# Moving the split weights of the half-width products by 144 bytes (112 for paired values) inside their buffers

## The chip, the cores and the metric

The kernel runs on one core of one Trainium2 chip. The metric is the device time of one execution in microseconds (us); lower is better. One core has a matrix engine, TensorE (PE in the profile, with its weight loads listed apart as PEld), and four more engines: VectorE (DVE), ScalarE (ACT), GpSimd (POOL) and SyncE (SP, which only issues transfers here). On-chip memory is SBUF, 128 partitions wide; an address below is a byte offset within a partition. Matrix products land in PSUM.

## The reference, cut to what matters

A two-layer decoder trunk over 512 tokens of width 1024, all in float32:

- layer 0 mixes tokens by attention in three groups of eight heads, with windows of 128, 512 and 2048 tokens at strides 1, 4 and 16; the three groups' outputs are merged by their softmax denominators and projected;
- layer 1 mixes tokens by causal means over 2, 4, 8 and 16 positions, with one small linear map for each channel group;
- after each mixer comes a SwiGLU feed-forward block of hidden width 2816, and before every block an RMS norm.

```python
x = x + dilated_attention_mixer(rmsnorm(x, attn_norm), w_qkv, w_attn_out)   # layer 0
x = x + (silu(h @ gate) * (h @ up)) @ w_down                                # after each mixer
x = x + pooling_mixer(rmsnorm(x, pool_norm), w_pool_in, w_pool_group, scale) # layer 1
return rmsnorm(x, final_norm)
```

Nearly all of the arithmetic is in products of activations with weights that are read once from HBM.

## The kernel before, in words

**Split operands.** A float32 product is made of three TensorE products in the reduced type `fp32r`. Every operand is split into a high part (ScalarE copies it, rounded) and a low part (VectorE subtracts the high part from the original); `split` at L81 to L83 does it. Then high by high, high by low and low by high are summed in PSUM.

**Weights.** Weights arrive by transfer in `raw` buffers and are split into buffers of five in turn: `whi` and `wlo`, each 128 x 1024 (`halfhi` and `halflo`, 128 x 512, two in turn). The class `Held` takes such a buffer. Loads and splits stand in two lists, and `pump` issues the next of them after products, as soon as a buffer is free, so that the weights are split some products ahead of their use.

**Two kinds of products.** `Product` (L259, L260, L262) multiplies a 128 x 128 block of weights with 512 columns of activations. `seven` calls `mult` (L374 to L376): for two outputs at a time the eight quarter products are replaced by seven (Strassen's scheme, in a form that shares sums), and each of the seven is four blocks of 128 x 128 weights against 256 columns. `values12` (L488 to L490) does the same for two value projections with the operands' roles exchanged: there the activations are the stationary operand (the one that is loaded into the array) and the weights are the moving one, 256 columns wide. The class `Pair` loads the four quarters, forms their sums and splits four sets of weights ("b", "s", "m", "l"). In this text the products of `mult` and `values12` are the half-width products.

**Where things lie.** Activations that are split lie in slots of 128 x 2 x 512, in the buffers of `x`, or in some buffers of the attention's pool. In the program before, every slot and every weight buffer begins at an address that leaves 128 when divided by 256, and the blocks inside them begin at multiples of 512 (weights) or 1024 bytes (activations). So the stationary and the moving operand of each half-width product begin at the same remainder modulo 256. Two pads, each called `shift`, one in the pool of temporaries and one in the feed-forward pool, lie ahead of the slots.

**Sums of squares.** `square` (L288 on) forms the sum of squares for the next norm: ScalarE squares a chunk into `sq` (two buffers), and VectorE adds it to the sum so far in a new `acc` buffer (two buffers).

**Order.** Every engine runs its instructions in the order in which the program writes them. The order of the products is written out in the loops; the splits of later weights are put among them by `pump`.

Of the kernel before, what the change touches and what calls it, by code (L numbers as in the profile page):

```python
# [8 lines left out]
F32 = mybir.dt.float32  # L9
F32R = mybir.dt.float32r  # L10
# [5 lines left out]
P = 128  # L16
S = 512
# [26 lines left out]
DOWN = (6, 5)  # L44
BUFS = {"w": 5, "half": 2, "raw": 4, "rawhalf": 2}
COLS = {"w": D, "half": D // 2, "raw": D, "rawhalf": D // 2}
FIXED = 12
SLOTS = 15
QK = [(0, 0), (0, 1), (1, 0), (1, 1), (2, 0), (2, 1)]
# [4 lines left out]
def trunk(ctx: ExitStack, tc: tile.TileContext, xT, norms, w_first, w_qk, w_qkp, w_v0, w_v0p, w_v12, w_out, w_pair, w_down, w_pin, w_pgrp,  # L54
          consts, ident_in, invcnt_in, outT, outR):
    nc = tc.nc
    cpool = ctx.enter_context(tc.tile_pool(name="cpool", bufs=1))
    wpool = ctx.enter_context(tc.tile_pool(name="wpool", bufs=1))
    tmp = ctx.enter_context(tc.tile_pool(name="tmp", bufs=2))
# [21 lines left out]
    def split(hi, lo, v):  # L81
        nc.scalar.activation(hi, v, AF.Copy)  # L82
        nc.vector.tensor_tensor(lo, v, hi.bitcast(F32), op=OP.subtract)  # L83
# [3 lines left out]
    class Held:  # L87


        def __init__(self, ring):  # L90
            self.live = True
            n = COLS[ring]
            if ring in ("w", "half"):
                self.t = [wpool.tile([P, n], F32R, tag=ring + c, name=ring + c, bufs=BUFS[ring]) for c in ("hi", "lo")]
            else:
                self.t = wpool.tile([P, n], F32, tag=ring, name=ring, bufs=BUFS[ring])
            rings[ring].append(self)
# [28 lines left out]
    class Pair:  # L126

        def __init__(self, src):  # L130
            self.src, self.w = src, {}
            loads.append((self, {"raw": 2, "rawhalf": 1}, self.load))

        def steps(self):
# [8 lines left out]
                                self.src[:, None, 3 * S:].to_broadcast([P, 2, S]), accum_op=OP.add)  # L143

        def blocks(self):
            self.w["b"] = Held("w")
            split(*self.w["b"].t, self.a.t)

        def sums(self):
            self.w["s"] = Held("w")  # L150
            split(*self.w["s"].t, self.b.t)

        def more(self):
            a, b = self.a.t, self.b.t
            nc.vector.tensor_add(a[:, :S], a[:, :S], b[:, :S])
            nc.vector.tensor_add(a[:, S:], a[:, S:], a[:, :S])
            self.b.done()
            self.w["m"] = Held("w")
            split(*self.w["m"].t, a)
            self.a.done()  # L160

        def last(self):
            self.w["l"] = Held("half")
            split(*self.w["l"].t, self.c.t)
            self.c.done()

# [10 lines left out]
                return  # L177
            steps.popleft()[2]()

    def pairs(*srcs):  # L180

        these = [Pair(src) for src in srcs]
        for parts in zip(*(p.steps() for p in these)):
            steps.extend(parts)
        units.append(these)
# [5 lines left out]
    def plain(*srcs):  # L191
        units.extend([Plain(src) for src in srcs])

    for h in range(HEADS):
        if h == 0:
            plain(*[w_qk[u] for u in range(len(QK) - NF)])
        for g in range(3):
            if h == 1 and g < NSOLO:
                plain(*[w_qk[len(QK) - NF + 2 * g + c] for c in range(2)])
            elif h:  # L200
                pairs(w_qkp[3 * h - 3 - NSOLO + g])
        if h == 0:
            plain(w_v0[0], w_v0[1])
        elif h % 2 == 0:
            pairs(w_v0p[h // 2 - 1])
        else:
            pairs(w_v12[h // 2, 0], w_v12[h // 2, 1])
    plain(*[w_out[m] for m in range(KC)])

    def ffn_plan(layer):  # L210
# [20 lines left out]
    class Product:  # L231
# [16 lines left out]
        def add(self, ks, cols=slice(0, S), pos=None):  # L248
            for k in ks:
                if self.w:  # L250
                    w, c = self.w, k if pos is None else pos + k
                else:
                    held, c = self.where(k)
                    w = held.t
                    if c == self.sizes[len(self.tiles) - 1] - 1 and not self.keep:
                        held.done()
                s = slice(c * P, (c + 1) * P)
                mh, ml = self.ins(k)
                nc.tensor.matmul(self.p[:, cols], w[0][:, s], mh[:, cols], start=self.done == 0, stop=False)  # L259
                nc.tensor.matmul(self.p[:, cols], w[0][:, s], ml[:, cols], start=False, stop=False)  # L260
                self.done += 1
                nc.tensor.matmul(self.p[:, cols], w[1][:, s], mh[:, cols], start=False, stop=self.done == self.n)  # L262
            if not self.w:
                pump(2)
            return self


    free, pools = deque(range(FIXED)), {i: cpool for i in range(FIXED)}

# [18 lines left out]
    acc = {}  # L288

    def square(layer, k, engine=None):  # L290
        sq = tmp.tile([P, S], F32, name="sq")
        nc.scalar.activation(sq, X[k], AF.Square)
        if layer not in acc:
            acc[layer] = sq
            return
        new = tmp.tile([P, S], F32, name="acc")
        (engine or nc.vector).tensor_add(new, acc[layer], sq)
        acc[layer] = new

    def scaled(layer, k, hi, lo, on_dve=False):  # L300

# [8 lines left out]
    def note(layer, k):  # L310

        if layer < 4:
            held[layer, k], t = slot("h")
            scaled(layer, k, t[:, 0], t[:, 1])
        square(layer, k)
# [67 lines left out]
    def seven(T, one, two, scratch, after={}, blocks=False):  # L383
# [35 lines left out]
        if blocks:  # L419
            for a in (left, right):  # L420
                nc.vector.tensor_add(in_place(sums, a), in_place(p73, a), into(one, right))
        else:
            nc.vector.tensor_add(sums, p73, again(one[:, H2:]))
# [32 lines left out]
    with tc.tile_pool(name="opool", bufs=1) as opool:  # L456
        early = opool.tile([P, HEADS, S], F32R, tag="o", name="early")
        with tc.tile_pool(name="apool", bufs=1) as apool:
# [6 lines left out]
            def scaled_by(t, p, blocks):  # L465
                nc.vector.tensor_mul(by_block(t) if blocks else t, p, rows["row"])
# [292 lines left out]
            for k in range(KC):  # L759
                if k % 2 == 0:  # L760
                    rawh, wh = Held("raw"), Held("w")
                    rawh.done()
                    wh.done()
                    raw, (hi, lo) = rawh.t, wh.t
                s = slice(k % 2 * NF * P, (k % 2 + 1) * NF * P)
                nc.sync.dma_start(X[k], xT[:, k, :])
                nc.sync.dma_start(raw[:, s], w_first[k])
                nc.scalar.activation(hi[:, s], raw[:, s], AF.Copy)
                scaled(0, k, *U[k], on_dve=k == 0)
                nc.vector.tensor_tensor(lo[:, s], raw[:, s], hi[:, s].bitcast(F32), op=OP.subtract)  # L770
                for i, f in enumerate(lead):
                    f.w = (hi, lo)
                    f.add([k], pos=k % 2 * NF + i - k)
                square(0, k)
# [79 lines left out]
            output(last - 1)  # L854
            halve(last - 1)
            turn0(last)
            turn12(last)
            lead.append(Product(HEADS, heads).add(range(last - 1)))
            output(last)
            halve(last)  # L860
            for f in lead:
# [14 lines left out]
    with tc.tile_pool(name="fpool", bufs=2) as fpool:  # L876
        fpool.tile([P, 32], F32, name="shift", bufs=1)
        for i in range(FIXED, FIXED + SLOTS):
            free.append(i)
# [160 lines left out]
        def mix(g):  # L1040
            for c in range(2):
                f = Product(2, lambda k: Y[g][k], w=wg[g // 2, g % 2]).add(range(2), pos=2 * c)
                m = 2 * g + c
                nc.vector.scalar_tensor_tensor(X[m], f.p, nrm[:, 5, m:m + 1], X[m],
                                               op0=OP.mult, op1=OP.add)
                held[3, m], t = slot("n")
                scaled(3, m, t[:, 0], t[:, 1])
                square(3, m, nc.gpsimd)
            for c in range(2):
                give(("y", g, c))  # L1050
# [23 lines left out]
        def end(i, half, js, f=None):  # L1074
            f = f or Product(HALF, hidden, keep=ends[i])
            return f.add(js, cols=halves[half])
# [38 lines left out]
        def total(half, sq):  # L1115
            t = ftile("total", H2)
            nc.vector.tensor_add(t, acc[4][:, halves[half]], sq)
            return t

        t = total(0, add(0, 0, end(0, 0, range(HALF))))  # L1120
        sq = add(1, 0, end(1, 0, range(HALF)))
# [3 lines left out]
        t = total(1, add(0, 1, f))  # L1125
# [6 lines left out]
        sq = add(1, 1, f)  # L1132
# [90 lines left out]
```

## Time and profile before

| | |
|---|---|
| median of 3 runs | 1249.99 us (1249.98 to 1250.75) |
| span of the profiled execution | 1249.2 us |
| TensorE products, weight loads | 9294, 9294 |
| TensorE busy | 99% of the span |
| VectorE busy | 922.7 us, 74% |
| ScalarE busy | 569.4 us, 46% |
| granted TensorE clock | 0.999 of full |

The profile gives one profiled execution; no time of that execution other than its span is given. An instruction of TensorE is listed with its start and a duration; products are pipelined, so that a listed duration (283 ns for 256 columns) is longer than the distance from one start to the next (0.12 us). How quickly TensorE works is therefore read from the distances of the starts in the timeline, or from how many products fall into a stretch of time. The trace holds starts in whole nanoseconds; the timeline rounds them to 0.01 us. Names such as `ps<-tt,whi` say that a product into PSUM read the tile `tt` (split activations) and `whi` (high parts of weights).

### The profile page before, as it was taken

To read this page: it belongs to the slowest core of one execution; us is meant where nothing else is said; L and a number is where in the kernel's file an instruction comes from. 1 tells how busy PE (TensorE), PEld (TensorE's weight loads), DVE (VectorE), ACT (ScalarE), POOL (GpSimd) and SP (SyncE) were. 2 spreads that over 40 slices of the span, in tenths; PEclk is the share of its full clock that TensorE was granted. 3 is DMA by queue.
4 is the path that set the end of the run, shared out by engine and by line. 5 is a ranking of instruction groups with operands and counts; after the bars stand their busy time and mean duration, and the time that the engine had idled before them with its cause. 6 is when DMAs were issued, how large, how long until landed. Compare 5 with 4: busy or idle time off the path is not lost.

```text
span 1249.2 us, 23008 instructions
## 1 busy us (share of the span) xinstructions
PE 1238.6 (99%) x9294; PEld 1141.3 (91%) x9294; DVE 922.7 (74%) x1474; ACT 569.4 (46%) x923; POOL 123.5 (10%) x119
## 2 busy tenths in 40 slices
PE   9999999999999999999999999999999999999998
PEld 7889999999999988899889999888789988999987
DVE  6888887877879754889437886659888954788643
ACT  6545464545446552545324554443444632455331
POOL 1011121111111100000001100000400000111000
PEclk9999999999999999999999999999999999999999
DMA  8346565666665633356356763333135645676321
GB/s 288 113 111 154 142 160 154 165 151 150 155 155 146 208 108 100 79 135 179 111 143 176 184 169 119 110 129 119 51 85 119 183 128 141 168 181 171 98 70 68
DMA packets 67307, 174.14 MB, mean 139 GB/s; under 512 B 6896, under 2 KB 8064, under 8 KB 67200
## 3 DMA queue, kind: packets, MB, share of 16 engines
q1 hardware_dynamic: 49248, 137.26, 33.6%
q0 software_dynamic: 17808, 35.14, 17.2%
q8 instruction: 73, 1.20, 0.4%
q14 instruction: 34, 0.28, 0.1%
q10 hardware_dynamic: 144, 0.26, 0.1%
HBM read 170.54 MB, written 2.10 MB: 138 GB/s over the span
## 4 chain that ended last, share of the span: by engine, by line
PE 80%; issue 11%; DVE 7%; POOL 1%; ACT 1%; DMA 0%; SPq 0%; DVEq 0%; POOLq 0%; ACTq 0%
PE ps L374 14%; PE ps L375 14%; PE ps L376 14%; PE ps L259 9%; PE ps L262 9%; PE ps L260 9%; PE ps L488 2%; PE ps L490 2%; PE ps L489 2%; DVE wlo L83 1%; PE ps L700 1%; DVE raw L437 1%; PE ps L572 1%; PE ps L592 1%; PE ps L694 1%
## 5 line engine op out<-in xcount | busy, mean ns | idle before, releaser
L82 ACT ACTIVATE whi<-raw 128x1024 fp32r<-128x1024 f32 (+2 forms) x299 | 297.4, 1001 | 404.1 <-PE ps L260 191.8
L83 DVE TENSOR_TENSOR wlo<-raw,whi 128x1024 fp32r<-128x1024 f32 (+2 forms) x299 | 342.8, 1150 | 163.2 <-ACT whi L82 162.0
L259 PE MATMUL ps<-a,whi 128*128 128x512 f32 (+1 forms) x374 | 141.1, 377 | 0.0
L260 PE MATMUL ps<-a,whi 128*128 128x512 f32 (+1 forms) x374 | 140.9, 377 | 0.0
L262 PE MATMUL ps<-a,wlo 128*128 128x512 f32 (+1 forms) x374 | 140.8, 376 | 0.0
L374 PE MATMUL ps<-tt,whi 128*128 128x256 f32 x408 | 115.5, 283 | 0.0
L375 PE MATMUL ps<-tt,whi 128*128 128x256 f32 x408 | 115.5, 283 | 0.0
L376 PE MATMUL ps<-tt,wlo 128*128 128x256 f32 x408 | 115.5, 283 | 0.0
L142 POOL DMA_DIRECT2D raw<-w_pair x34 | 41.1, 1209 | 439.3 <-DVE wlo L83 191.0
L262 PEld LDWEIGHTS ps<-a,wlo 128*128 128x128 f32 x374 | 70.4, 188 | 12.9
L259 PEld LDWEIGHTS ps<-a,whi 128*128 128x128 f32 x374 | 70.4, 188 | 12.8
L260 PEld LDWEIGHTS ps<-a,whi 128*128 128x128 f32 x374 | 70.4, 188 | 12.8
L374 PEld LDWEIGHTS ps<-tt,whi 128*128 128x128 f32 x408 | 78.3, 192 | 0.0
L375 PEld LDWEIGHTS ps<-tt,whi 128*128 128x128 f32 x408 | 78.3, 192 | 0.0
L376 PEld LDWEIGHTS ps<-tt,wlo 128*128 128x128 f32 x408 | 78.3, 192 | 0.0
L375 PE MATMUL ps<-tb,whi 128*128 128x256 f32 x272 | 77.2, 284 | 0.1
L376 PE MATMUL ps<-tb,wlo 128*128 128x256 f32 x272 | 77.0, 283 | 0.0
L374 PE MATMUL ps<-tb,whi 128*128 128x256 f32 x272 | 76.9, 283 | 0.0
L374 PE MATMUL ps<-h,whi 128*128 128x256 f32 x252 | 72.7, 289 | 0.0
L376 PE MATMUL ps<-h,wlo 128*128 128x256 f32 x252 | 71.3, 283 | 0.0
L375 PE MATMUL ps<-h,whi 128*128 128x256 f32 x252 | 71.2, 283 | 0.0
L259 PE MATMUL ps<-h,whi 128*128 128x512 f32 x144 | 56.4, 392 | 0.0
(281 smaller groups left out, 3363.6 us busy)
## 6 DMA issues: line engine op xcount, KB each, us to landing
raw<-w_pair SPq DMA_DIRECT2D x78, 512.0 KB, 4.2
raw<-w_qkp SPq DMA_DIRECT2D x36, 512.0 KB, 4.5
raw<-w_pair POOLq DMA_DIRECT2D x34, 512.0 KB, 7.4
raw<-w_down SPq DMA_DIRECT2D x32, 384.0 KB, 3.1
raw<-w_down SPq DMA_DIRECT2D x32, 320.0 KB, 2.8
raw<-w_v SPq DMA_DIRECT2D x18, 512.0 KB, 4.4
raw<-w_qkp POOLq DMA_DIRECT2D x18, 512.0 KB, 7.0
rawhalf<-w_pair SPq DMA_DIRECT2D x34, 256.0 KB, 3.3
```

The source lines that it names most:

```text
L82: nc.scalar.activation(hi, v, AF.Copy)
L83: nc.vector.tensor_tensor(lo, v, hi.bitcast(F32), op=OP.subtract)
L142: nc.gpsimd.dma_start(self.b.t.rearrange("p (a c) -> p a c", a=2), self.src[:, None, 3 * S:].to_broadcast([P, 2, S]), accum_op=OP.add)
L259: nc.tensor.matmul(self.p[:, cols], w[0][:, s], mh[:, cols], start=self.done == 0, stop=False)
L260: nc.tensor.matmul(self.p[:, cols], w[0][:, s], ml[:, cols], start=False, stop=False)
L262: nc.tensor.matmul(self.p[:, cols], w[1][:, s], mh[:, cols], start=False, stop=self.done == self.n)
L374: nc.tensor.matmul(dst, w.t[0][:, c], th, start=k == 0, stop=False)
L375: nc.tensor.matmul(dst, w.t[0][:, c], tl, start=False, stop=False)
L376: nc.tensor.matmul(dst, w.t[1][:, c], th, start=False, stop=k == K2 - 1)
L488: nc.tensor.matmul(o, mh, wh, start=k == 0, stop=False)
L489: nc.tensor.matmul(o, mh, wl, start=False, stop=False)
L490: nc.tensor.matmul(o, ml, wh, start=False, stop=k == K2 - 1)
```

## The change

The high and the low parts of a set of weights now lie in one buffer that has 64 elements (256 bytes) to spare, and a set can begin some elements into it. Weights of half-width products begin 36 elements (64 - 28, 144 bytes) into the buffer; those of the paired values (`values12`), which are the moving operand, begin 28 elements (112 bytes) into it. The moving operand's address less the stationary operand's is then 112 modulo 256 in both. Weights of the 512-column products begin at 0 as before. The seven buffers take 7 x 256 = 1,792 bytes more of each partition.

To make room, `square` keeps its sum in the `sq` buffer (three buffers) instead of separate `acc` buffers: three buffers of 2,048 bytes where there were four. Tiles that lie behind the temporaries move by 256 bytes in all (1,792 - 2,048), which leaves their remainders modulo 256 as they were.

```diff
+LINE = 64
+APART = 28
 class Held:
-    def __init__(self, ring):
+    def __init__(self, ring, shift=0):
         if ring in ("w", "half"):
-            self.t = [wpool.tile([P, n], F32R, tag=ring + c, name=ring + c, bufs=BUFS[ring]) for c in ("hi", "lo")]
+            t = wpool.tile([P, 2 * n + LINE], F32R, tag=ring, name=ring, bufs=BUFS[ring])
+            self.t = [t[:, shift + i * n:shift + (i + 1) * n] for i in range(2)]
...
 class Pair:
     def blocks(self):
-        self.w["b"] = Held("w")
+        self.w["b"] = Held("w", self.shift)
...
-def pairs(*srcs):
+def pairs(*srcs, shift=LINE - APART):
...
-            pairs(w_v12[h // 2, 0], w_v12[h // 2, 1])
+            pairs(w_v12[h // 2, 0], w_v12[h // 2, 1], shift=APART)
...
 def square(layer, k, engine=None):
-    sq = tmp.tile([P, S], F32, name="sq")
+    sq = tmp.tile([P, S], F32, name="sq", bufs=3)
     nc.scalar.activation(sq, X[k], AF.Square)
-    if layer not in acc:
-        acc[layer] = sq
-        return
-    new = tmp.tile([P, S], F32, name="acc")
-    (engine or nc.vector).tensor_add(new, acc[layer], sq)
-    acc[layer] = new
+    if layer in acc:
+        (engine or nc.vector).tensor_add(sq, acc[layer], sq)
+    acc[layer] = sq
```

More of the change, by code (lines that the diff above doesn't have):

```diff
@@ L126, in trunk, with __init__ @@
     class Pair:
-        def __init__(self, src):
-            self.src, self.w = src, {}
+        def __init__(self, src, shift):
+            self.src, self.shift, self.w = src, shift, {}
             loads.append((self, {"raw": 2, "rawhalf": 1}, self.load))
@@ L145, in blocks @@
         def blocks(self):
-            self.w["b"] = Held("w")
+            self.w["b"] = Held("w", self.shift)
             split(*self.w["b"].t, self.a.t)
         def sums(self):
-            self.w["s"] = Held("w")
+            self.w["s"] = Held("w", self.shift)
             split(*self.w["s"].t, self.b.t)
@@ L157, in more @@
             self.b.done()
-            self.w["m"] = Held("w")
+            self.w["m"] = Held("w", self.shift)
             split(*self.w["m"].t, a)
@@ L162, in last @@
         def last(self):
-            self.w["l"] = Held("half")
+            self.w["l"] = Held("half", self.shift)
             split(*self.w["l"].t, self.c.t)
@@ L178, in pump @@
             steps.popleft()[2]()
-    def pairs(*srcs):
-        these = [Pair(src) for src in srcs]
+    def pairs(*srcs, shift=LINE - APART):
+        these = [Pair(src, shift) for src in srcs]
         for parts in zip(*(p.steps() for p in these)):
```

## The prediction

> **What bounds the kernel now.** I read the page's busy time first, then TensorE's waits, then the windows of a stage that has only half-width products, then the timeline in which single products start.
>
> ```profile
> span 1249.2 us, 23008 instructions
> PE 1238.6 (99%) x9294; PEld 1141.3 (91%) x9294; DVE 922.7 (74%) x1474; ACT 569.4 (46%) x923; POOL 123.5 (10%) x119
> ```
>
> ```profile
> engine line waited for: us in total, times, longest us
> PE ps L260 <- DVE n L307: 1.5, 2, 0.7
> PE ps L758 <- DVE idle L755: 1.2, 1, 1.2
> PE ps L259 <- ACT y L82: 0.7, 1, 0.7
> PE ps L337 <- POOL rcol L330: 0.6, 2, 0.4
> PE ps L262 <- DVE wlo L770: 0.2, 1, 0.2
> ```
>
> TensorE is busy for 99% of the span, and all that it is seen to wait for adds up to 4.2 us. So the time is the number of products times the distance between their starts, and no other engine's time enters unless TensorE begins to wait. The next rows count the half-width products of one of the three lines of `mult` and of one of the three of `values12`, and after that show a stage that has nothing else in it.
>
> ```profile
> 0.00:1249.20 1249.20, 438.82 (x1540) 295.30 (x1540) 1.00 0.51 139
> ...
> 0.00:1249.20 1249.20, 63.96 (x224) 1.00 0.51 139
> ```
>
> ```profile
> core 0: us, PE busy (x) PEld busy (x) DVE busy (x) ACT busy (x) POOL busy (x), PEclk, DMA share, GB/s
> 720.00:740.00 20.00, 20.00 (x169) 20.00 (x168) 17.28 (x25) 10.33 (x14) 2.44 (x2) 1.00 0.71 183
> ```
>
> L374 has 1,540 products (with their loads beside them) and L488 has 224 (its row lists the products alone); L375, L376 and L489, L490 are written in the same loops, so the half-width products are 3 x (1,540 + 224) = 5,292. In 20 us some 168 of them start: 20,000 / 168 = 119 ns each. The granted clock is 1.00, so no throttle takes part. The timeline gives the distance more closely:
>
> ```profile
> 582.02 0.28 PE L375 MATMUL ps<-tb,whi 128*128 128x256 f32 x1
> ...
> 583.22 0.28 PE L376 MATMUL ps<-tt,wlo 128*128 128x256 f32 x1
> ```
>
> The second of these rows is the tenth product after the first: (583.22 - 582.02) / 10 = 0.120 us. So 5,292 x 0.120 = 635 us, half of the kernel, is paced by this one distance, and **one nanosecond of it is worth 5.3 us**, 0.42% of the time.
>
> Is the 120 ns a fixed price, or does it depend on how the read of the next weights falls on the read of the moving operand? Two more places speak to that. The first is half-width products just after other work has broken the rhythm, the second is 512-column products, first after a break and then settled.
>
> ```profile
> 131.16 0.28 PE L375 MATMUL ps<-t,whi 128*128 128x256 f32 x1
> ...
> 131.87 0.28 PE L375 MATMUL ps<-tx,whi 128*128 128x256 f32 x1
> ```
>
> ```profile
> 290.57 0.29 PE L374 MATMUL ps<-h,whi 128*128 128x256 f32 x1
> 290.70 0.28 PE L375 MATMUL ps<-h,whi 128*128 128x256 f32 x1
> 290.81 0.28 PE L376 MATMUL ps<-h,wlo 128*128 128x256 f32 x1
> ```
>
> ```profile
> 600.13 0.40 PE L260 MATMUL ps<-a,whi 128*128 128x512 f32 x1
> ...
> 601.06 0.39 PE L262 MATMUL ps<-a,wlo 128*128 128x512 f32 x1
> 601.29 0.39 PE L259 MATMUL ps<-a,whi 128*128 128x512 f32 x1
> ...
> 605.82 0.39 PE L262 MATMUL ps<-a,wlo 128*128 128x512 f32 x1
> ```
>
> After the break there are six intervals from 131.16 to 131.87, 0.118 us each. At 290.57 one interval is 0.13 and the next 0.11 (125 and 113 ns by the trace's whole-nanosecond starts). Of all 5,292 intervals, 270 are such loose ones, neither 120 ns nor a stop, with a mean of 118.5 ns between 113 and 125. For 512 columns it is the other way round: four intervals from 600.13 to 601.06 take 0.232 us each, the settled ones from 601.29 to 605.82 (twenty) 0.227. The shapes, tiles and addresses modulo 256 are the same before and after settling. So the distance is not a fixed price of changing weights. It depends on the phase in which two reads run beside each other, by several nanoseconds in both directions, and it settles into a fixed phase. An address offset between the two operands is another way to shift that phase, so the change can reach the bound.
>
> **The change part by part.**
>
> *The offset of 112 between the operands of half-width products.* No row shows this offset: every half-width product of this run has offset 0 modulo 256. The bounds come from the loose intervals: the best, 113 ns, gives 5,292 x (113 - 120) = -37 us; the worst, 125 ns, gives 5,292 x 5 = +26 us. Their mean, 118.5, gives -8 us: that would be an offset without any system to it. I take 116 ns, about half-way between the mean and the best: with the operands nearly half a period of 256 apart, I expect the settled phase to be a good one and not an average one. That is 5,292 x -4 = **-21 us**.
>
> *Data that start at an odd place.* ScalarE and VectorE now write the split weights at a start that is a multiple of 16 bytes and no longer of 128. The rows of the pooling sums bound that, whose inputs are shifted by 4 bytes (from `u`) and 8 to 32 bytes (from `s`):
>
> ```profile
> L1027 DVE TENSOR_TENSOR s<-s x12: 671/685/687, 851.4 to 877.9; 128x512 f32<-128x512 f32 x12
> L1027 DVE TENSOR_TENSOR s<-u x8: 672/674/1051, 849.6 to 889.9; 128x512 f32<-128x512 f32 x8
> ```
>
> Their medians, 674 and 685 ns, don't grow with the odd start. I take 0; those are reads, so for writes I keep an end of 10% of VectorE's 17.28 us in 20, 1.7 us, which still fits in the 20.
>
> *Whether the others follow.* A Strassen unit has 7 x 12 = 84 products, 84 x 0.120 = 10.08 us now. VectorE's work in that time is 17.28 / 20 x 10.08 = 8.71 us. At 116 ns the unit takes 9.74 us and VectorE is busy for 89% of it; at 113 ns, 9.49 us and 92%. It would become the bound at 8.71 / 84 = 104 ns, below every row here; with the 10% of the paragraph above, at 114 ns. The DMA share of 0.71 grows to 0.73. So I take nothing off, and keep up to 5 us (a quarter of the gain) in the range for waits at the seams between stages.
>
> *High and low parts in one buffer.* A buffer now comes free for ScalarE's next split only after the low part's last product and not already after the high part's, which in `mult` and `Product` is the product before: one distance, 0.12 to 0.23 us later. Behind that split in ScalarE's queue stand the next splits, Silu and the copies of `first`, for which VectorE waits. TensorE has no row in which it waits for a split of pumped weights (the list above is complete; L770 is the very first block), so several buffers stand between; I take 0. Without that cover it would be up to 0.23 us for each of the 235 full splits, 54 us.
>
> ```profile
> L83 DVE TENSOR_TENSOR wlo<-raw,whi 128x1024 fp32r<-128x1024 f32 x235 | 286.0, 1221 | 98.3 <-ACT whi L82 97.8
> ```
>
> *The sums of squares in place.* Before, chunk k was squared into the buffer of chunk k-2, free once addition k-2 had read it. Now it goes into the buffer that holds the sum after addition k-3, which addition k-2 reads. The wait is for the same addition, and the addition reads and writes as much as before: 0. GpSimd's additions in the pooling layer (L297) follow the same rule.
>
> *What stays.* The 512-column products keep offset 0, and tiles behind the temporaries move by a multiple of 256.
>
> The sum against the profiled span: 1249.2 - 21 = 1228 us; the runs' median is 0.8 us above the span, so **1229 us**.
>
> **A rule against this.** The Trainium skill, "TensorE: Matmul & The Clock Gate", section "Step-by-step: what each phase is for", says that the array has two separate SBUF read ports, one for each operand, and that loading the next weights takes no read bandwidth from the running product. By that rule an offset between the two can do nothing, and the sum would be 1250. The trace disagrees at least in part: 0.232 and 0.227 us for the same product with nothing but the phase between them. The same page, section "Back-to-back issue gap", gives N / 2.4 + 2.5 ns between isolated products; as an estimate by that, 256 columns would take 109 ns and the sum would be 1249.99 - 5,292 x 0.011 = 1192 us.
>
> **The rivals.**
>
> *The offset does nothing: 1250 us.* The phase that settles could be fixed by the start times alone, whatever the addresses: all settled distances are exactly alike, in slots from all over the memory. Two kinds of float32 products speak for it: L694's weights lie 64 bytes off the other operand modulo 256, L700's 0, and their durations agree.
>
> ```profile
> L700 PE MATMUL ps<-t,v 128*128 128x128 f32 x128 | 15.6, 275 | 0.0
> L694 PE MATMUL ps<-t,v 128*128 128x128 f32 x64 | 12.3, 274 | 0.0
> ```
>
> Against it: these are float32 products, which go through the array twice (the first row counts 128 where the code has 64), so that reads meet differently, and the loose intervals show that phase matters.
>
> *The offset settles into a worse phase: 1276 us.* The 512-column rows show that another phase can cost 5 ns over the settled one. If offset 112 puts half-width products there, at 125 ns, the price is +26 us. It decides from 120.5 ns on: half a nanosecond is 2.6 us, 0.2%. For it: the present addresses give the best settled phase for 512 columns, and may be good for 256 too. Against it: for 256 columns the loose phases are on average better than the settled one.
>
> *The distance falls so far that VectorE becomes the bound.* At 109 to 112 ns the products alone would give 1192 to 1208 us; VectorE then is 8.71 / 9.2 = 95% busy and its chains (product, sums, Silu, split) show as waits. I expect some 1210 us here, beside the best bound above.
>
> **How the numbers follow.** A faster settled distance: 0.66, of which 0.10 for the last rival; taken alone this case reaches from 1203 to 1245. Nothing changes: 0.08. A worse phase: 0.26. A measurement of this kernel tells 0.2%, 2.5 us, from no change. The prediction is the likeliest case, 1229. Below, 0.08 stay out at 1203. Above, the range takes in no change and the worse phases up to 123 ns (5,292 x 3 = 16 us, 1266), ending at 1268, which leaves out some 0.12.
>
> **What would show it.** In the same stage the starts of ten successive half-width products span about 1.16 us and not 1.20, 20 us hold some 172 of them and not 168, and VectorE's share rises to 89%. 512-column products stay at 0.227. TensorE's list of waits stays near 4 us; a row for `whi` or for PSUM in it would mean that VectorE or ScalarE doesn't follow. Writes at odd starts would show as longer splits than 1221 ns. The prediction is wrong if the settled distance is again 0.120 or above it.

## The result, and the profile after

The changed kernel takes 1245.15 us (median of 4, 1243.47 to 1245.23), the kernel before took 1250.23 beside it: a ratio of 0.9953, 95% interval 0.9939 to 0.9967. It is faster, by 5 us and not by 21.

The page and TensorE's list of waits of the changed kernel:

```profile
span 1241.7 us, 22947 instructions
PE 1231.7 (99%) x9294; PEld 1135.8 (91%) x9294; DVE 922.1 (74%) x1474; ACT 572.5 (46%) x923; POOL 125.9 (10%) x119
```

```profile
engine line waited for: us in total, times, longest us
PE ps L758 <- DVE idle L755: 1.2, 1, 1.2
PE ps L263 <- DVE n L307: 0.9, 2, 0.6
PE ps L337 <- POOL rcol L330: 0.9, 2, 0.5
PE ps L263 <- DVE s L1025: 0.7, 1, 0.7
```

TensorE still waits for next to nothing (3.7 us), so the result is again a sum of distances between starts. The profiled execution is the fastest of the four: its run took 1243.47 us, 1.8 us more than its span. The timeline shows three paces. First an ordinary Strassen unit of the first feed-forward layer (ten intervals), then one of the second layer (twelve), then the paired values (twelve):

```profile
582.05 0.28 PE L374 MATMUL ps<-tt,w 128*128 128x256 f32 x1
...
583.25 0.28 PE L375 MATMUL ps<-tn,w 128*128 128x256 f32 x1
```

```profile
959.83 0.28 PE L374 MATMUL ps<-tt,half 128*128 128x256 f32 x1
...
961.23 0.28 PE L374 MATMUL ps<-tb,w 128*128 128x256 f32 x1
```

```profile
309.93 0.28 PE L488 MATMUL ps<-w,tx 128*128 128x256 f32 x1
...
311.29 0.28 PE L488 MATMUL ps<-w,tx 128*128 128x256 f32 x1
```

That is 0.120 us, 0.117 us and 0.113 us for products of the same shape with the same distance of 112 bytes modulo 256 between their operands. Only the last two are faster than before. In whole-nanosecond starts the first alternates between 119 and 121, the second goes 117, 117, 116, and the third 113, 113, 114. The same stretch as in the prediction (the first row) holds as many products as before. The second row lies among the first six units of the second layer: VectorE is busy there all the time, as it is in the same stretch before the change, and TensorE waits for nothing.

```profile
core 0: us, PE busy (x) PEld busy (x) DVE busy (x) ACT busy (x) POOL busy (x), PEclk, DMA share, GB/s
720.00:740.00 20.00, 20.00 (x169) 20.00 (x168) 17.31 (x24) 10.52 (x15) 2.44 (x2) 1.00 0.70 181
970.00:990.00 20.00, 20.00 (x174) 20.00 (x173) 20.00 (x29) 12.91 (x18) 1.21 (x1) 1.00 0.70 184
```

Adding up all distances between starts in the two traces gives where the time went. Means leave out the long stops.

| products | number | before, us (mean ns) | after, us (mean ns) |
|---|---|---|---|
| `mult`, the ordinary Strassen units | 4,620 | 558.3 (119.92) | 556.0 (119.38) |
| `values12`, the paired values | 672 | 81.2 (119.93) | 77.2 (113.95) |
| 512 columns | 2,238 | 514.8 (226.97) | 512.4 (226.92) |
| all others | 1,763 | 87.2 | 88.5 |

The paired values are an eighth of the half-width products and bring 4.0 us; the other seven eighths bring 2.4 us. (The 512-column products keep their pace; their 2.4 us are a few stops at stage ends, and 1.3 of it goes back among the others.) Of the 34 feed-forward units, 28 still run at 120.0 and the first six of the second layer at 116.67; the means of the attention's units lie between 118.3 and 120.0. The six units at 116.67 save 504 x 3.3 = 1.7 us, which is also what the profiled run is below the median, so the other runs may lack them; no trace of those runs was kept.

So the questions are: which part of the change brought the 5 us; why does one and the same distance of operands give 113 ns in one place and 120 in another; and is there an address at which all half-width products run at 113?

### The profile page after: what moved, and what is told of

The parts are those of the page before. It is cut to its first block, busy times and chain, and to the rows that moved or that the text cites. A ratio compares the mean times of both kernels' runs of the same rounds, so it can differ in the third digit from the quotient of the medians.

```text
span 1241.7 us, 22947 instructions
## 1 busy us (share of the span) xinstructions
PE 1231.7 (99%) x9294; PEld 1135.8 (91%) x9294; DVE 922.1 (74%) x1474; ACT 572.5 (46%) x923; POOL 125.9 (10%) x119
## 4 chain that ended last, share of the span: by engine, by line
PE 89%; DVE 8%; issue 2%; ACT 0%; POOL 0%; DVEq 0%; POOLq 0%; DMA 0%; ACTq 0%
PE ps L374 15%; PE ps L375 15%; PE ps L376 15%; PE ps L262 11%; PE ps L263 11%; PE ps L265 11%; PE ps L488 2%; PE ps L490 2%; PE ps L489 2%; DVE w L85 2%; PE ps L700 1%; DVE raw L437 1%; PE ps L572 1%; DVE n L307 1%; PE ps L592 1%
## 5 line engine op out<-in xcount | busy, mean ns | idle before, releaser
L84 ACT ACTIVATE w<-raw 128x1024 fp32r<-128x1024 f32 (+2 forms) x299 | 297.5, 1001 | 410.9 <-PE ps L265 171.2
L85 DVE TENSOR_TENSOR w<-raw,w 128x1024 fp32r<-128x1024 f32 (+2 forms) x299 | 343.0, 1151 | 162.6 <-ACT w L84 161.2
L262 PE MATMUL ps<-a,w 128*128 128x512 f32 (+1 forms) x374 | 141.0, 377 | 0.0
L263 PE MATMUL ps<-a,w 128*128 128x512 f32 (+1 forms) x374 | 140.8, 377 | 0.0
L265 PE MATMUL ps<-a,w 128*128 128x512 f32 (+1 forms) x374 | 140.8, 377 | 0.0
L374 PE MATMUL ps<-tt,w 128*128 128x256 f32 x408 | 115.7, 284 | 0.0
L375 PE MATMUL ps<-tt,w 128*128 128x256 f32 x408 | 115.7, 284 | 0.0
L376 PE MATMUL ps<-tt,w 128*128 128x256 f32 x408 | 115.7, 284 | 0.0
L265 PEld LDWEIGHTS ps<-a,w 128*128 128x128 f32 x374 | 70.4, 188 | 13.0
L262 PEld LDWEIGHTS ps<-a,w 128*128 128x128 f32 x374 | 70.4, 188 | 12.9
L263 PEld LDWEIGHTS ps<-a,w 128*128 128x128 f32 x374 | 70.4, 188 | 12.6
L375 PE MATMUL ps<-tb,w 128*128 128x256 f32 x272 | 77.3, 284 | 0.1
L374 PEld LDWEIGHTS ps<-tt,w 128*128 128x128 f32 x408 | 77.4, 190 | 0.0
L375 PEld LDWEIGHTS ps<-tt,w 128*128 128x128 f32 x408 | 77.4, 190 | 0.0
L376 PEld LDWEIGHTS ps<-tt,w 128*128 128x128 f32 x408 | 77.4, 190 | 0.0
L374 PE MATMUL ps<-tb,w 128*128 128x256 f32 x272 | 77.1, 283 | 0.0
L376 PE MATMUL ps<-tb,w 128*128 128x256 f32 x272 | 77.1, 283 | 0.0
L374 PE MATMUL ps<-h,w 128*128 128x256 f32 x252 | 72.8, 289 | 0.0
L376 PE MATMUL ps<-h,w 128*128 128x256 f32 x252 | 71.3, 283 | 0.0
L375 PE MATMUL ps<-h,w 128*128 128x256 f32 x252 | 71.3, 283 | 0.0
L262 PE MATMUL ps<-h,w 128*128 128x512 f32 x144 | 56.5, 392 | 0.0
```

The lines of the kernel that those rows point to most:

```text
L374: nc.tensor.matmul(dst, w.t[0][:, c], th, start=k == 0, stop=False)
L375: nc.tensor.matmul(dst, w.t[0][:, c], tl, start=False, stop=False)
L376: nc.tensor.matmul(dst, w.t[1][:, c], th, start=False, stop=k == K2 - 1)
```

## Experiments

### Each part alone

In one kernel the ordinary units' weights go back to shift 0; in another all shifts are 0, and only the common buffers and the sums in place are left.

```diff
-    def pairs(*srcs, shift=LINE - APART):
+    def pairs(*srcs, shift=0):
...
-            pairs(w_v12[h // 2, 0], w_v12[h // 2, 1], shift=APART)
+            pairs(w_v12[h // 2, 0], w_v12[h // 2, 1], shift=0)    # the second kernel only
```

> The changed kernel with the shift of 112 bytes for the paired values alone and 0 for the ordinary Strassen units. By the traces the paired values' 672 products save 672 x 6.0 ns = 4 us, and the 4,620 others 2.5 us. If the gain is the sum of the two: 1246.3 us, a ratio of 0.9968 to before, and slower than the changed kernel by 1 to 2.5 us. If the paired values carry all of it: 1245. If the shift of the ordinary units does harm in some stage: below 1245.

> The changed kernel with all shifts 0: only the common buffer for both parts, the 256 bytes to spare and the sums of squares in place are left. My steps put these at nothing: 1250.2, a ratio of 1.000 within 0.002. If the buffers coming free later did cost something, hidden by the gain in the result: up to 1252. If the sums in place or the moved buffers are what gained: 1245.

With the paired values shifted alone: 1246.34 us, ratio 0.9960 (0.9947 to 0.9974). With no shift: 1250.31 beside 1250.88, ratio 0.9995 (0.9986 to 1.0004). So the new buffers and the sums in place cost and bring nothing that can be measured. The paired values bring nearly all of the change's gain: their interval and the changed kernel's (0.9939 to 0.9967) overlap, and the ordinary units' 144 bytes are worth 1.2 us between the two medians, which these runs don't tell from nothing. In the trace of the first kernel the two kinds are at 119.91 and 113.93 ns.

### A sweep with the weights as loaded operand

Each of the 17 Strassen units of a feed-forward layer gets its own shift, so that one trace holds a table.

```diff
-                    pairs(w_pair[layer, j])
+                    n = j - NPLAIN
+                    pairs(w_pair[layer, j], shift=(4 * n if layer == 0 else 60 - 4 * n) % LINE)
```

> The changed kernel, but each of the 17 Strassen units of a feed-forward layer has its own weight shift: 0, 16, 32, ... 240 bytes and 0 again in the first layer, the same in falling order (240 down to 0, then 240) in the second. In these units the weights are the loaded operand and the activations (remainder 128 modulo 256) the moving one. Theory 'distance' (the settled distance of starts is a function of the operands' distance modulo 256 alone): each shift gives its own settled distance, the same in both layers; 0 bytes gives 120.0 ns as before, 144 bytes gives something between 116.7 and 120, and some other shift gives the 113.3 ns of the paired values. Theory 'entry' (the distance that a run of products settles into depends on the phase in which it begins, and the shift only sets how many such rhythms there are): the same shift gives different distances in the two layers, with no smooth dependence. Theory 'no role for the address': 120 throughout.

Settled means in ns (products 25 to 80 of a unit), by the shift in bytes:

| shift | layer 0 | layer 1 | | shift | layer 0 | layer 1 |
|---|---|---|---|---|---|---|
| 0 | 120.0, 120.0 | 120.0 | | 128 | 118.7 | 118.6 |
| 16 | 118.3 | 118.3 | | 144 | 120.0 | 120.0 |
| 32 | 118.3 | 118.3 | | 160 | 120.0 | 120.0 |
| 48 | 117.7 | 118.3 | | 176 | 118.1 | 118.1 |
| 64 | **113.3** | 117.8 | | 192 | 117.8 | **113.3** |
| 80 | 118.8 | 118.6 | | 208 | 116.7 | 116.7 |
| 96 | 117.3 | 118.7 | | 224 | 116.7 | 116.7 |
| 112 | 120.0 | 120.0 | | 240 | 120.0 | 117.3, 120.0 |

The address does set the pace: twelve of sixteen shifts give the same mean in both layers, within about 0.6 ns. But 64, 192, 96 and 240 bytes have two means each. "Entry" fits these, "distance" the rest; since only the weights are moved here, the sweep can't tell the distance from the weights' own place. And 144 bytes, the change's own choice, is among the worst of the table: as slow as no shift. The time of this kernel is 1240.41 us (one run, as for all sweeps and the kernels with moved activations or a moved base below), less than the changed kernel's, with one unit in sixteen at each address.

### A sweep with the weights as moving operand

The paired values' four sets of weights have a shift each in each of the four calls, and the 512-column down projections are swept too; ordinary units stay at 0.

```diff
-            pairs(w_v12[h // 2, 0], w_v12[h // 2, 1], shift=APART)
+            pairs(w_v12[h // 2, 0], w_v12[h // 2, 1], shift=tuple(16 * (h // 2) + 4 * i for i in range(4)))
...
-                plain(src[:, :DOWN[0] * P], src[:, DOWN[0] * P:])
+                n = hf * KC + m
+                plain(src[:, :DOWN[0] * P], src[:, DOWN[0] * P:], shift=4 * n if layer == 0 else 60 - 4 * n)
```

> Weights of the ordinary Strassen units at shift 0 again. In the paired values, where the weights are the moving operand and the activations are loaded, the 16 sets of weights (4 calls, 4 sets each) have shifts of 0, 16, ... 240 bytes. And the weights of the 512-column down projections have 0, 16, ... 240 bytes in layer 0 and falling in layer 1. Theory 'distance': the paired values show at the shift s the distance that the first sweep shows at the shift 256 - s, since moving less loaded is then the same; 113.3 ns at 112 bytes. Theory 'role' (what counts is where the moving operand begins, 240 modulo 256 in the paired values and 128 in the others): the two sweeps don't mirror each other. For 512 columns both expect 226.7 at 0; if the address matters there, values between 216 and 236 appear at other shifts.

Means by the distance moving less loaded (for the ordinary units, 256 less the shift):

| distance | ordinary units | paired values | | distance | ordinary units | paired values |
|---|---|---|---|---|---|---|
| 32 | 116.7 | 116.7 | | 48 | 116.7 | 118.3 |
| 64 | 117.8, 113.3 | 115.6 | | 80 | 118.1 | 119.8 |
| 96 | 120.0 | 120.0 | | **112** | **120.0** | **113.3** |
| 128 | 118.6 | 118.7 | | 144 | 120.0 | 118.7 |
| 160 | 117.3, 118.7 | 117.3 | | 176 | 118.7 | 119.0 |
| 192 | 113.3, 117.8 | 114.1 | | 208 | 117.7, 118.3 | 119.2 |
| 224 | 118.3 | 118.3 | | 240 | 118.3 | 117.4 |

(The left half has the multiples of 32 but 0, the right half odd multiples of 16 but 16, at which ordinary units show 120.0 and 117.3 and the paired values 118.8; sets of the paired values are short, 24 to 48 products, so their means hold some of the run-in.) Where the distance is a multiple of 32, the paired values agree with the ordinary units or with one of their two means, at 64 and 192 apart from the run-in: the last products of these sets start every 113.3 ns. At odd multiples of 16 they differ, by 0.3 ns at 176 and most of all, by 6.7, at 112. So the distance does not decide alone; where each operand lies counts too. The table says a little more. At distance d an ordinary unit has its operands at remainders 128 - d and 128, the paired values at 128 and 128 + d: the same pair, moved by d. So in these rows a move of both operands by a multiple of 32 bytes leaves the pace as it is, and a move by an odd multiple of 16 mostly doesn't.

For 512 columns, shifts of 0 and 16 bytes are best, with 227.5 and 226.9 ns (in this sweep each occurs once). With shifts from 32 bytes on the means lie between 228.6 and 234.3 ns, as in these rows (nine intervals of 0.233 us), and the kernel takes 1253.73 us:

```profile
621.29 0.39 PE L267 MATMUL ps<-a,w 128*128 128x512 f32 x1
...
623.39 0.40 PE L267 MATMUL ps<-a,w 128*128 128x512 f32 x1
```

### The same distance, but where the paired values have it

If places count, then ordinary units should run at 113 when their loaded operand begins at remainder 128 and their moving one at 240, as in the paired values. So the weights stay at 0 and the activations of the feed-forward units begin 112 bytes into larger slots.

```diff
-LINE = 64
+LINE = 0
...
-        i = free.popleft()
-        t = pools[i].tile([P, 2, S], dtype, tag=f"slot{i}", name=name, bufs=1)
-        return i, t
+        late = name in ("tb", "tt", "tn")
+        i = next((i for i in free if (i >= FIXED) == late), free[0])
+        free.remove(i)
+        if i < FIXED:
+            return i, pools[i].tile([P, 2, S], dtype, tag=f"slot{i}", name=name, bufs=1)
+        t = pools[i].tile([P, 2 * S + 64], dtype, tag=f"slot{i}", name=name + "on" if late else name, bufs=1)
+        o = APART if late else 0
+        return i, t[:, o:o + 2 * S].rearrange("p (e s) -> p e s", e=2)
```

> Weights at shift 0 everywhere (paired values too). Instead, in the feed-forward layers, the split activations of the Strassen units (the moving operand there) begin 112 bytes into their slots, so that moving less loaded is 112 as in the paired values and in the changed kernel, with the loaded operand at remainder 128 and the moving one at 240 as in the paired values. The sums of squares have two buffers. Read the settled distance of the feed-forward units alone. Theory 'where the moving operand begins': 113.3 ns as in the paired values, and never 120. Theory 'distance and entry alone' (places don't count, only the difference and the phase): 120, 118.3 or 116.7 ns as in the changed kernel. Theory 'role of the weights': likewise not 113.3.

All 17 units of the first layer settle at 113.33 ns and stay there (ten intervals of 0.113 us):

```profile
689.90 0.28 PE L381 MATMUL ps<-tton,w 128*128 128x256 f32 x1
...
691.03 0.28 PE L379 MATMUL ps<-tton,w 128*128 128x256 f32 x1
```

In the second layer one activation tile (`tt` in the profile, where the others are `tbon`, `tton` and `tnon`) had no large slot, and the units average 115.1. Its three products in a set start every 118 ns, and the products behind them, at the good addresses again, do not return to 113 at once:

```profile
981.64 0.28 PE L379 MATMUL ps<-tton,w 128*128 128x256 f32 x1
...
982.95 0.28 PE L381 MATMUL ps<-tton,w 128*128 128x256 f32 x1
```

These eleven intervals take 119 ns each. In the layer's units after the first the mean of such eleven is 118.6, without a stop, and 113.3 follows. So for a while the pace at given addresses depends on which products ran just before. "Where the moving operand begins" is borne out in the first layer, and the role of the weights is not what counts: they are the loaded operand here. The kernel takes 1233.95 us, with the attention's units and the paired values at shift 0.

### Is it the moving operand's place alone?

> The kernel in which the activations of the feed-forward Strassen units begin 112 bytes into their slots, but three of the four sets of weights of these units (b, s, m; 6 of 7 products) begin 112 bytes into their buffers too: both operands at remainder 240, difference 0. One buffer fewer for scratch tiles of the feed-forward. Read the first feed-forward layer's products of these sets. If the start of the moving operand (240) decides by itself: 113.3 ns. If the difference decides: 120.0 as before the change. If both count: something else.

```diff
-                    pairs(w_pair[layer, j])
+                    pairs(w_pair[layer, j], shift=APART)
...
-            self.w["l"] = Held("half", self.shift)
+            self.w["l"] = Held("half")
```

(The edit is against the kernel of the last experiment, with room again in the `w` buffers, one scratch buffer fewer and a pad that keeps the remainders.) The moving operand begins at 240 in all products of a unit. For six of the seven the loaded one begins at 240 too, for the last at 128. First the six (ten intervals), then the last one (eleven), in one trace:

```profile
569.90 0.28 PE L379 MATMUL ps<-tbon,w 128*128 128x256 f32 x1
...
571.08 0.28 PE L380 MATMUL ps<-tbon,w 128*128 128x256 f32 x1
```

```profile
557.95 0.28 PE L379 MATMUL ps<-tton,half 128*128 128x256 f32 x1
...
559.19 0.28 PE L381 MATMUL ps<-tton,half 128*128 128x256 f32 x1
```

0.118 and 0.113 us. The rows come from two units, but 15 of the layer's 17 units go the same way: 118.3 ns in the products with both at 240, then 113.3 in the last twelve. The other two units, each the first one behind products of 512 columns, run at 116.7 with the pair (240, 240), so that this pair has two paces as well. The kernel takes 1242.48 us. So the moving operand's place doesn't decide by itself, and difference 0 isn't always 120 either. Both operands' places count together.

### Everything moved by 128 bytes

> The changed kernel with everything moved up by 128 bytes: the ordinary Strassen units have the loaded operand at remainder 144 and the moving one at 0 modulo 256 (before: 16 and 128), the paired values 0 and 112 (before: 128 and 240). All differences are as in the changed kernel. If remainders modulo 128 are what counts, or only differences: 120, 118.3 and 116.7 ns in the ordinary units and 113.3 in the paired values, as in the changed kernel, 1244 to 1246 us. If remainders modulo 256 count: other rhythms in either, and 1220 to 1255.

```diff
+    cpool.tile([P, 32], F32, name="base")
     X = [x_tile(k) for k in range(KC)]
```

1244.03 us, with nearly the paces of the changed kernel: the paired values at 113.3 (mean 113.95 in both), 28 feed-forward units at 120.0, the attention's units unit by unit as there. Only the first six units of the second layer differ, 118.3 where the changed kernel has 116.7; both were named as its paces beforehand. So the places count modulo 128, or in a way that this shift leaves as it is. 128 is a multiple of 32, so this agrees with the table of the two sweeps; other moves of both operands were not tried by themselves.

### Better addresses for the ordinary units

From the sweep 64 and 208 bytes were tried for all ordinary units, and then a sweep in steps of 4 bytes was made.

```diff
-    def pairs(*srcs, shift=LINE - APART):
+    def pairs(*srcs, shift=16):    # 64 bytes; 52, 13 and 19 elements in the other kernels
```

> The changed kernel with 64 bytes instead of 144 as the shift of the ordinary Strassen units' weights (paired values stay at 112). In the first sweep a unit at 64 bytes ran at 113.3 ns in one layer and at 117.8 in the other. If the distance of the operands decides which rhythms exist: between 4,620 x (119.9 - 117.8) = 10 us and 4,620 x 6.6 = 30 us less than the 1246.3 of the kernel with shifted paired values alone, so 1216 to 1237; runs may differ by which rhythm they settle into. If units only ran so because of what stood before them in the sweep: 1243 to 1246.

> The same with 208 bytes, which gave 116.66 ns in both layers of the first sweep. If that rhythm is the only one there: 4,620 x (119.92 - 116.66) = 15 us less than 1246.3, so 1231, with runs alike within 1 us; the settled starts show 7 products in 0.817 us. If what stood before a unit decides: 1240 to 1246.

64 bytes: 1230.29 us, ratio 0.9835 (0.9818 to 0.9851). 208 bytes: 1231.59, ratio 0.9846 (0.9829 to 0.9862). At 208 all units run at 116.7, as the sweep said. At 64, all 34 feed-forward units settled in the slower of the two paces, 117.8, and the attention's units, which are broken into by other work, moved between 113.3 and 117.8 (mean 114.8).

> The first sweep in steps of 4 bytes: the 17 units of a feed-forward layer have shifts of 48, 52, ... 80 and 192, 196, ... 220 bytes, in falling order in the second layer. If reads go by 16-byte lines: steps within 16 bytes change nothing, and the distances move at 48, 64, 80, 192 and 208 alone. If each 4 bytes of distance count: a gradual or saw-tooth course of settled distances between 113 and 120. If the entry decides: no agreement between the layers.

| shift, bytes | 48 | 52 | 56 | 60 | 64 | 68 | 72 | 76 | 80 |
|---|---|---|---|---|---|---|---|---|---|
| layer 0 | 117.8 | **113.3** | 118.0 | 119.7 | **113.3** | 118.3 | 118.4 | **113.3** | 118.8 |
| layer 1 | 117.8 | **113.3** | 117.8 | 119.4 | 117.8 | 118.3 | 118.4 | **113.3** | 118.8 |

The kernel takes 1239.46 us. Four bytes are enough to change the pace, so this is no matter of 16-byte steps; the course is neither gradual nor a saw-tooth. (From 192 to 220 bytes the means are 116.7 to 120.8; 200 bytes has two paces, 120.0 and 116.7, and none has 113.3, not even 192 bytes, which had it in one layer of the first sweep.)

> The changed kernel with 52 bytes as the shift of the ordinary Strassen units' weights (paired values at 112). In the fine sweep units at 52 bytes settled at 113.33 ns in both layers. If a shift that settles so from two different entries settles so from every entry: 4,620 x (119.9 - 113.5) = 30 us less than the 1246.3 with shifted paired values alone, so 1216 to 1219, and VectorE must follow at 8.7 us of work in a unit of 9.5 us. If other entries lead to other rhythms, as at 64 bytes: 1222 to 1234. If VectorE becomes the bound: settled starts of 113.3 with stops between them, and waits of TensorE for w or PSUM in its list.

> The same with 76 bytes, the other shift that settled at 113.33 ns in both layers of the fine sweep: 1216 to 1219 if every entry settles so, 1222 to 1234 if some don't. If the two good shifts are good for the same reason, the two kernels lie within 2 us of each other.

52 bytes: 1234.8 us, ratio 0.9873 (0.9858 to 0.9888). 76 bytes: **1216.71 us, ratio 0.9726 (0.9710 to 0.9743)**, beside 1250.92 before, the best kernel of this study. Two addresses alike in the sweep are 18 us apart in use. The windows show where. First the kernel with 52 bytes, in two stages of one layer:

```profile
550.00:570.00 20.00, 20.00 (x179) 20.00 (x178) 19.50 (x28) 12.53 (x17) 2.41 (x2) 1.00 0.80 204
690.00:710.00 20.00, 20.00 (x169) 20.00 (x169) 17.29 (x24) 10.55 (x15) 2.41 (x2) 1.00 0.71 181
```

The first six units of each layer run at 113.3, the other eleven, behind the down projections, at 120.0, at the same addresses. Two sweep entries did not tell that a third entry leads to another pace. (That the products before them make the difference is argued: VectorE and the transfers are busier in the first stage too, and no run varies them alone.) With 76 bytes both stages run at 113.3; the page and the window of that kernel:

```profile
PE 1205.7 (99%) x9294; PEld 1109.5 (91%) x9294; DVE 921.1 (76%) x1474; ACT 572.7 (47%) x923; POOL 125.9 (10%) x119
```

```profile
690.00:710.00 20.00, 20.00 (x179) 20.00 (x178) 18.37 (x27) 11.64 (x16) 2.43 (x2) 1.00 0.74 193
```

178 products in 20 us, where the kernel with 52 bytes has 169 in the same stretch. VectorE is busy for 92% of this stage and TensorE's list of waits still has only the same kinds of rows, 4.0 us in all: the others follow.

```profile
PE ps L758 <- DVE idle L755: 1.2, 1, 1.2
PE ps L337 <- POOL rcol L330: 1.2, 3, 0.5
PE ps L263 <- DVE n L307: 0.9, 2, 0.6
PE ps L263 <- DVE s L1025: 0.7, 1, 0.7
```

## Why the prediction was right or wrong

**The bound** held. In every kernel TensorE's waits stay between 3.3 and 4.8 us, and the time follows the distances of starts: 5,292 times a nanosecond is 5.3 us. With 76 bytes, 4,620 x (119.92 - 113.57) = 29 us less than 1246.34 would be 1217; 1216.71 was measured. (113.57 is the mean of its attention and feed-forward units: 113.88 and 113.39, weighted by 1,764 and 2,856.)

**That the 120 ns are not a fixed price** held: addresses alone make 113 to 120 ns of them. No settled pace of any run lies below 113, the best loose interval, and the worst, at a shift of 220 bytes, is 120.8. That the lower end fits so well is luck. In the trace of before, each of the 13 intervals of 125 ns, the one at 290.57 among them (114 follows there by the trace, not 113), is followed by one of 113 or 114, and these are 13 of the 18 so short: a late start made up for, and not a pace.

**The step that failed** is the size of the one term that mattered: "I take 116 ns, about half-way between the mean and the best: with the operands nearly half a period of 256 apart, I expect the settled phase to be a good one and not an average one". Only the first six units of the second layer come near it, with 116.67. The measured mean is 119.38 for the 4,620 ordinary products and 113.95 for the 672 paired values. 4,620 x -0.54 is -2.5 us and 672 x -5.98 is -4.0: -6.5 in the sum of the profiled run instead of -21, and -5.1 between the medians. In 28 of 34 feed-forward units the settled distance is again 0.120, which the prediction had named as the sign of its being wrong. That the kernel got faster as forecast is owed mostly to the paired values, one eighth of the products, at whose places this distance happens to be a good one. Two assumptions in that sentence were wrong. The first is that the two kinds of products, with the same distance, would have one pace; the sweeps and the moved activations show that places count beside the distance. The second is that half a period apart is good: for ordinary units 128 bytes gives 118.6 and 144 gives 120.0, while 76 gives 113.3. Nothing in the trace of before held either of them, since every half-width product there had one distance and one remainder. The loose intervals gave bounds and could not give the place between them.

**The smaller terms** held. New buffers and sums in place: 1250.31 against 1250.88, where 0 was taken. Writes at odd starts: a full split on VectorE takes 1222 ns in the changed kernel and 1223 with 76 bytes, against 1221, so the 10% kept for it was not needed. The later release of buffers: ScalarE idles 285 us ahead of the full splits instead of 282, and TensorE has no row for it.

**The rivals.** "The offset does nothing" was given 0.08 and describes 28 of 34 feed-forward units, though not for its reason: other offsets do a great deal. "A worse phase" hardly occurs for 256 columns (120.8 at 220 bytes is the slowest); it is what 512 columns show, 228.6 to 234.3 ns at shifts from 32 bytes on. "VectorE becomes the bound" did not occur, even with 92% at 113.3 ns, the share the prediction worked out for 113, nor in the stretch of the changed kernel where VectorE is busy all the time.

**The rule** of the Trainium skill ("TensorE: Matmul & The Clock Gate", "Step-by-step: what each phase is for"), that loading the next weights takes no read bandwidth from the running product, would leave the pace alone, and here it does not stay: with the ordinary units' weights begun 76 bytes later, their products start every 113.3 ns instead of 120.0. The prediction's picture of two reads that meet in a phase fits this, but no run shows what the reads share.

**What stays open.** Why a pair of places gives the pace that it gives; the runs show that it depends on both operands' places in steps of 4 bytes, that 128 bytes added to both change next to nothing, and that several pairs have two or three paces. Products just before decide for some eleven products, as the moved activations show; that what ran before also chooses a pace that lasts fits the sweeps and the kernel with 52 bytes, but the other engines' accesses were never varied apart from it. Whether 76 bytes holds for all entries was seen only in this kernel's order of work.

## What to carry to other kernels

When TensorE runs without waits, divide a stage's time by its products: if the starts are several per cent further apart than the best ones in the same trace, the addresses of the two operands are worth a sweep, and giving each unit its own offset puts a whole table into one run. Take the offset from the kernel's own products and roles, not from another shape: what is best for one (112 bytes for the paired values) was worth nothing for another, and harmful for 512 columns. Then time the whole kernel, because the pace of an address can differ from place to place in the program: 52 and 76 bytes were equal in the sweep and 18 us apart in use.

## What was not expected of the hardware

Products of 256 columns settle into exact paces, most often 113.33, 116.67, 118.33 or 120.00 ns on average (117.79 in all 34 feed-forward units with 64 bytes), in short repeating patterns of intervals (119, 121; or 120, 121, 118, 115). One pair of addresses can have several: the changed kernel shows 120.0, 118.3 and 116.7 at the same addresses in one execution. Kernels with several paces varied more from run to run, in four runs each: 1232.7 to 1236.9 us with 52 bytes and 1227.9 to 1232.1 with 64, against 1216.2 to 1217.9 with 76 and 1231.2 to 1231.9 with 208.
